# Swapping the 256-column and the 512-column matmuls inside three of the seven products of a Strassen pair

## The chip, the cores and the metric

The kernel runs on one core of one Trainium2 chip. The metric is device time in microseconds (us) for one execution; lower is better. Besides TensorE (PE), which runs the matmuls and loads their weights (PEld in the profile), the core has VectorE (DVE), ScalarE (ACT), GpSimd (POOL) and SyncE (SP), each with its own queue worked off in order, and 16 DMA engines.

## The reference

One layer of a token mixer over 512 frames of width 2048, in float32. One combined projection of the normalised input feeds three attention branches of four heads, and three gates; the branches are projected back, weighted by the gates, summed and projected once more.

```python
proj = jnp.einsum('bsd,dc->bsc', hn, w_in)            # 512 x 2048 by 2048 x 12292
br = proj[..., :QKVG_COLS].reshape(b, s, N_BRANCH, 4, BRANCH_W)      # q, k, v, gate path per branch
gates = jax.nn.sigmoid(proj[..., QKVG_COLS + N_HEADS:] + b_gate).reshape(b, s, N_BRANCH, D_MODEL)
...
ys = ys * jax.nn.silu(br[:, :, :, 3])                  # ys: the three branches' attention outputs
up = jnp.einsum('bsnw,nwd->bsnd', ys, w_up)
merged = jnp.sum(gates * up, axis=2)
return x + jnp.einsum('bsd,de->bse', merged, w_out)
```

Almost all of the arithmetic is in the two einsums with `w_in` and `w_out`, and the change is in how these are run.

## The kernel before

**Precision by two parts.** A float32 operand is cut into a high part (ACT copies it into a rounded type, line 244) and a low part (DVE subtracts the high part from the original, line 248). For weights these are the tiles `wh` and `wl`, each 128x1024, that is eight 128x128 blocks; for activations a tile `x`, `t` or `m` holds, for each of its halves, 256 high columns and then 256 low columns side by side. A product of a weight block and an activation half is then two matmuls, both issued at line 263:

- a **wide** one, `wh` by 512 columns (256 high, 256 low), into the whole of a PSUM tile `acc`,
- a **narrow** one, `wl` by the 256 high columns alone, into the left half of the same tile.

Left and right half of `acc` are added later.

**Seven products for a pair.** `PairTask` computes two output column tiles at once by a Strassen scheme: the contraction (2048) and the frames (512) are each cut in two, and seven products, numbered 1 to 7, take the place of eight. A product is eight weight blocks, so eight wide matmuls and eight narrow ones. The order of the products is

```python
self.order = (1, 5, 2, 3, 6, 7, 4) if late else (1, 2, 6, 5, 7, 3, 4)
```

All pairs but two have `late` false. In these, products 6, 7, 4 and 3 add onto the PSUM tile of an earlier product (`onto`, and with it `more` being true): 6 onto 1, 7 onto 6, 4 onto 7, 3 onto 5. The weights of product 6 are those of 1 plus those of 5 (a DVE add, line 626), and those of 3 are those of 2 plus that sum (line 632). There are 50 such pairs, 350 products: query, key, value and gate columns of eleven heads, most merge gates, and at the end the output projection. Activations `x` and `t` belong to the input projection, `m` to the output projection.

**What sets the order.** The kernel writes its own order for PE, ACT and DVE. A planner (`Flow`) holds generators; each yields an engine and an assumed cost, an event, or free slots, and the planner lets the one that could start first issue its next instruction. The main stream (`stream`) walks through the products one by one. When it comes to product i it starts `prep` of product i+2, which allocates `wh` and `wl` (three buffers of each) and yields the two splits. After a product, `after_of` reads the PSUM tile out. The attention of the heads (transposes at line 971 of the probabilities `p`, scores, values) is spread between as side work.

```python
def prep(u):
    n = u.shape[0] * P
    u.hi = wp.tile([P] + u.shape, F32R, tag="wh", name=nm("wh"), bufs=LA + 1)
    u.lo = wp.tile([P] + u.shape, F32R, tag="wl", name=nm("wl"), bufs=LA + 1)
    yield u.source_there()
    yield from split(u.hi, u.lo, u.source(), n, u.ready, hi_ev=u.ready_hi)
```

`ready_hi` is set after the ACT instruction, `ready` after the DVE one. `stream` waits for `ready_hi` ahead of a product, and the product itself waits for `ready` ahead of its narrow matmuls.

Of the kernel before, what the change touches and what calls it, by code (L numbers as in the profile page):

```python
# [16 lines left out]
S = 512  # L17
# [8 lines left out]
UK = 8  # L26
NQ = 4
HS = S // 2
# [8 lines left out]
PE, ACT, DVE = 0, 1, 2  # L37
# [112 lines left out]
def mm_us(n, x=1):  # L150
    return x * max(0.115, n / 2400 + 0.0133)
# [11 lines left out]
def hybrid_kernel(  # L163
# [40 lines left out]
    def acc(i=0):  # L204

        return pa.tile([P, S], F32, tag=f"acc{i}", name=nm("acc"), bufs=1 if i else 2)
# [10 lines left out]
    LH, RH = slice(0, HS), slice(HS, S)  # L217

    def two(ap):

        return ap.rearrange("p (h s) -> p h s", h=2)
# [40 lines left out]
    def mm(ps, w, x, start=False, stop=False, more=False):  # L262
        nc.tensor.matmul(ps, w, x, start=start, stop=stop, skip_group_check=more)  # L263
# [324 lines left out]
    class PairTask:  # L588
# [52 lines left out]
        def mms_of(self, i):  # L641
            p = self.order[i]
            bank = (0, 1, 2, 0, 0, 1, 2)[i] if self.late else {2: 1, 5: 2, 3: 2}.get(p, 0)
            onto = None if self.late else {6: 1, 7: 6, 4: 7, 3: 5}.get(p)
            more = onto is not None
            self.bank = getattr(self, "bank", {})
            self.bank[p] = bank

            def go(u):
                if more:  # L650
                    yield self.ev[onto]
                    self.ps[p] = self.ps[onto]
                else:
                    yield accs[bank], 1
                    self.ps[p] = acc(bank)

                for j in range(UK):
                    yield lambda: self.ops[p](j) is not None
                    r, _, ev = self.ops[p](j)
                    yield ev  # L660
                    yield PE, mm_us(S)
                    mm(two(self.ps[p]), u.hi[:, j, :], r, j == 0 and not more, more=more)
                yield u.ready
                for j in range(UK):
                    yield PE, mm_us(HS)
                    mm(self.ps[p][:, LH], u.lo[:, j, :], self.ops[p](j)[1], stop=j == UK - 1, more=more)
            return go

        def after_of(self, i):
# [875 lines left out]
```

## Time and profile before

| | |
|---|---|
| time, median of 3 runs | 1346.16 us (1345.8 to 1347.92) |
| the profiled execution: its time | 1346.45 us |
| the profiled execution: span of its instructions | 1344.7 us |
| granted TensorE clock, mean | 0.997 |
| PE busy | 1328.4 us, 7406 matmuls |
| DVE busy | 1112.7 us, 1624 instructions |
| ACT busy | 792.7 us, 1214 instructions |
| low splits of weights on DVE (line 248) | 412, 1200 ns each |
| high splits of weights on ACT (line 244) | 412, 1038 ns each |

The span runs from the first to the last instruction; the time is 1.75 us more. A matmul's row gives the time from its start until its result has been drained, and the next one starts before that: durations of matmuls overlap, and their pace is read from their starts. Where rows of a timeline are merged, `x8` behind a row is the number of instructions in it.

### The profile page before, as it was taken

The numbers are of one execution on the slowest core, as the hardware profiler recorded it, in microseconds if no ns is written. First come the engines' busy times: TensorE is split into PE (matmuls) and PEld (weight loads), VectorE is DVE, ScalarE is ACT, GpSimd is POOL, SyncE is SP. The second block draws the span as 40 slices with busy tenths as digits, with TensorE's granted clock in tenths as the row PEclk, the third lists the DMA queues.
The fourth block names the chain that finished last, engine by engine and source line by source line (L and its number), as shares of the span: only waits on it lengthen the run. The fifth ranks groups of instructions, "written<-read, shape, count | busy, mean of one in ns | idle before, by whom it ended". The sixth has DMA issues, their size and how long they took to land.

```text
span 1344.7 us, 19813 instructions
## 1 busy us (share of the span) xinstructions
PE 1328.4 (99%) x7406; PEld 1151.6 (86%) x7406; DVE 1112.7 (83%) x1624; ACT 792.7 (59%) x1214; POOL 91.3 (7%) x115
## 2 busy tenths in 40 slices
PE   9999999999999999999999999999999999989998
PEld 7788888888888888888888888888888788878887
DVE  5998998978888788787887878878798877898786
ACT  6745656656565566655766557665567655454443
POOL 0000000010000100000000000100000000001000
PEclk9999999999999999999999999999999999989999
DMA  9566767767777677777767777767767655658883
GB/s 328 176 154 158 190 165 195 181 188 203 186 200 195 180 215 182 185 206 184 214 171 190 203 194 199 176 191 198 194 193 257 238 197 188 187 146 242 235 250 91
DMA packets 91600, 263.03 MB, mean 196 GB/s; under 512 B 10216, under 2 KB 16488, under 8 KB 91504
## 3 DMA queue, kind: packets, MB, share of 16 engines
q1 hardware_dynamic: 72928, 202.97, 44.9%
q0 software_dynamic: 14976, 54.53, 24.8%
q10 hardware_dynamic: 3600, 4.26, 0.9%
q8 instruction: 58, 0.95, 0.3%
q14 instruction: 38, 0.31, 0.1%
HBM read 242.04 MB, written 19.69 MB: 195 GB/s over the span
## 4 chain that ended last, share of the span: by engine, by line
PE 97%; DVE 1%; DMA 0%; ACT 0%; issue 0%; SPq 0%; DVEq 0%; ACTq 0%
PE acc L263 84%; PE att L263 9%; PE att L971 1%; PE att L1074 1%; PE att L1075 1%; PE att L259 1%; PE att L260 1%; PE att L258 1%; DVE wl L248 1%; PE att L1073 1%; DMA x<-in_xT 0%; PE att L1034 0%; PE att L875 0%; PE att L874 0%; DVE m L248 0%; ACT wh L244 0%
## 5 line engine op out<-in xcount | busy, mean ns | idle before, releaser
L248 DVE TENSOR_TENSOR wl<-raw,wh 128x1024 fp32r<-128x1024 f32 (+1 forms) x412 | 494.2, 1200 | 146.8 <-ACT wh L244 144.3
L244 ACT ACTIVATE wh<-raw 128x1024 fp32r<-128x1024 f32 (+1 forms) x412 | 427.0, 1038 | 146.5 <-PE acc L263 70.8
L263 PE MATMUL acc<-x,wh 128*128 128x512 f32 x1600 | 415.5, 395 | 1.0 <-ACT wh L244 1.0
L263 PEld LDWEIGHTS acc<-x,wh 128*128 128x128 f32 x1600 | 286.0, 189 | 53.1 <-ACT wh L244 1.1
L263 PE MATMUL acc<-t,wh 128*128 128x512 f32 x1056 | 271.6, 394 | 0.0
L263 PEld LDWEIGHTS acc<-x,wl 128*128 128x128 f32 x1504 | 210.5, 190 | 19.0
L263 PE MATMUL acc<-x,wl 128*128 128x256 f32 (+1 forms) x1504 | 223.4, 289 | 0.0
L263 PEld LDWEIGHTS acc<-t,wh 128*128 128x128 f32 x1056 | 188.1, 189 | 32.1
L263 PEld LDWEIGHTS acc<-t,wl 128*128 128x128 f32 x1056 | 145.3, 190 | 11.0
L263 PE MATMUL acc<-t,wl 128*128 128x256 f32 x1056 | 149.2, 282 | 0.0
L279 POOL DMA_DIRECT2D raw<-in_w_col x88 | 76.1, 864 | 932.7 <-DMA raw<-in_w_col 446.5
L263 PE MATMUL acc<-m,wh 128*128 128x512 f32 x448 | 113.8, 396 | 6.3 <-DVE m L248 5.9
L263 PEld LDWEIGHTS acc<-m,wh 128*128 128x128 f32 x448 | 81.5, 191 | 21.6 <-DVE m L248 6.3
L742 ACT ACTIVATE c<-acc 128x256 f32<-128x256 f32 x50 | 19.2, 383 | 97.3 <-PE acc L263 92.2
L263 PE MATMUL att<-y,wh 128*128 128x512 f32 x256 | 66.5, 390 | 1.3 <-DVE y L248 1.3
L720 ACT ACTIVATE u<-acc 128x512 f32<-128x512 f32 x50 | 29.8, 595 | 64.3 <-PE acc L263 64.2
L263 PEld LDWEIGHTS acc<-m,wl 128*128 128x128 f32 x448 | 61.9, 193 | 5.2 <-DVE wl L248 0.8
L632 DVE TENSOR_TENSOR raw<-raw,raw 128x1024 f32<-128x1024 f32 x52 | 63.5, 1222 | 0.4
L626 DVE TENSOR_TENSOR raw<-raw,raw 128x1024 f32<-128x1024 f32 x52 | 63.4, 1220 | 0.4
L263 PE MATMUL acc<-m,wl 128*128 128x256 f32 x448 | 63.4, 285 | 0.4 <-DVE wl L248 0.4
L703 ACT ACTIVATE v<-acc 128x512 f32<-128x512 f32 x52 | 31.1, 599 | 50.8 <-PE acc L263 47.5
L263 PEld LDWEIGHTS att<-y,wh 128*128 128x128 f32 x256 | 47.9, 188 | 12.3 <-DVE y L248 2.5
(179 smaller groups left out, 1374.0 us busy)
## 6 DMA issues: line engine op xcount, KB each, us to landing
raw<-in_w_col SPq DMA_DIRECT2D x236, 512.0 KB, 4.3
raw<-in_w_col POOLq DMA_DIRECT2D x88, 512.0 KB, 6.3
raw<-in_w_out SPq DMA_DIRECT2D x40, 512.0 KB, 4.7
gl<-c SPq DMA_DIRECT2D x48, 256.0 KB, 2.2
raw<-in_w_up SPq DMA_DIRECT2D x32, 384.0 KB, 3.4
sg<-gl SPq DMA_DIRECT2D x48, 256.0 KB, 5.4
raw<-in_w_out POOLq DMA_DIRECT2D x16, 512.0 KB, 7.2
x<-in_xT SPq DMA_DIRECT2D x16, 256.0 KB, 6.8
```

Source lines behind the costliest of these rows:

```text
L244: nc.scalar.activation(hi, src, AF.Copy)
L248: nc.vector.tensor_sub(lo, src, f(hi))
L258: nc.tensor.matmul(ps, lh, rh, start=start, stop=False, skip_group_check=more)
L259: nc.tensor.matmul(ps, lh, rl, start=False, stop=False, skip_group_check=more)
L260: nc.tensor.matmul(ps, ll, rh, start=False, stop=stop, skip_group_check=more)
L263: nc.tensor.matmul(ps, w, x, start=start, stop=stop, skip_group_check=more)
L279: nc.gpsimd.dma_start(to, src, accum_op=ALU.add)
L626: nc.vector.tensor_add(w[1], w[1], w[5])
L632: nc.vector.tensor_add(w[2], w[2], w[1])
L703: nc.scalar.activation(self.v, ps, AF.Copy)
L720: nc.scalar.activation(self.u, ps, AF.Copy)
L742: nc.scalar.activation(c, ps[:, RH], AF.Copy, scale=-1.0)
```

## The change

In a pair that is not `late`, products 6, 7 and 4 run their eight narrow matmuls first and their eight wide ones last. Products 1, 2, 5 and 3 stay wide first. So product 2 (ending narrow) meets 6 (beginning narrow), 6 (ending wide) meets 5 (beginning wide), 5 meets 7 narrow to narrow, 7 meets 3 wide to wide, 3 meets 4 narrow to narrow, and 4 meets product 1 of the next pair wide to wide. Each of the three must now have its low split before its first matmul, where it needed the high split alone.

```diff
-                for j in range(UK):
-                    yield lambda: self.ops[p](j) is not None
-                    r, _, ev = self.ops[p](j)
-                    yield ev
-                    yield PE, mm_us(S)
-                    mm(two(self.ps[p]), u.hi[:, j, :], r, j == 0 and not more, more=more)
-                yield u.ready
-                for j in range(UK):
-                    yield PE, mm_us(HS)
-                    mm(self.ps[p][:, LH], u.lo[:, j, :], self.ops[p](j)[1], stop=j == UK - 1, more=more)
+                def wide(last):
+                    for j in range(UK):
+                        yield lambda: self.ops[p](j) is not None
+                        r, _, ev = self.ops[p](j)
+                        yield ev
+                        yield PE, mm_us(S)
+                        mm(two(self.ps[p]), u.hi[:, j, :], r, j == 0 and not more, last and j == UK - 1, more=more)
+
+                def narrow(last):
+                    yield u.ready
+                    for j in range(UK):
+                        yield lambda: self.ops[p](j) is not None
+                        _, r, ev = self.ops[p](j)
+                        yield ev
+                        yield PE, mm_us(HS)
+                        mm(self.ps[p][:, LH], u.lo[:, j, :], r, stop=last and j == UK - 1, more=more)
+                for step, last in ((narrow, False), (wide, True)) if p in (6, 7, 4) and more else (
+                        (wide, False), (narrow, True)):
+                    yield from step(last)
```

Nine lines are added above most of the code, so line 971 of before is line 980 of the changed kernel, and 712, 688, 1020 are 721, 697, 1029.

**An undisturbed junction.** On PE, around product 4 of an early pair (weights `wh_1420`, `wl_1421`; it ends that pair, and `wh_1446` begins the next one), the order before has narrow, wide, narrow, wide:

```order
L263 MATMUL acc_1392<-x_17_127,wl_1391 128x256
L263 MATMUL acc_1294<-t_120_960,wh_1420 128x512 x2
L263 MATMUL acc_1294<-t_124_980,wh_1420 128x512 x2
L263 MATMUL acc_1294<-t_129_1027,wh_1420 128x512 x2
L263 MATMUL acc_1294<-t_132_1037,wh_1420 128x512 x2
L263 MATMUL acc_1294<-t_120_960,wl_1421 128x256 x2
L263 MATMUL acc_1294<-t_124_980,wl_1421 128x256 x2
L263 MATMUL acc_1294<-t_129_1027,wl_1421 128x256 x2
L263 MATMUL acc_1294<-t_132_1037,wl_1421 128x256 x2
L263 MATMUL acc_1501<-x_2_112,wh_1446 128x512
```

In the changed kernel the same place on PE has narrow, narrow, wide, wide:

```order
L263 MATMUL acc_1392<-x_17_127,wl_1391 128x256
L263 MATMUL acc_1294<-t_120_960,wl_1421 128x256 x2
L263 MATMUL acc_1294<-t_124_980,wl_1421 128x256 x2
L263 MATMUL acc_1294<-t_129_1027,wl_1421 128x256 x2
L263 MATMUL acc_1294<-t_132_1037,wl_1421 128x256 x2
L263 MATMUL acc_1294<-t_120_960,wh_1420 128x512 x2
L263 MATMUL acc_1294<-t_124_980,wh_1420 128x512 x2
L263 MATMUL acc_1294<-t_129_1027,wh_1420 128x512 x2
L263 MATMUL acc_1294<-t_132_1037,wh_1420 128x512 x2
L263 MATMUL acc_1500<-x_2_112,wh_1446 128x512
```

Only the two groups of product 4 have changed places. Over the whole program the order of PE goes from narrow to wide at 387 places before and at 229 in the changed kernel, from wide to narrow at 388 and 231.

**An early product 6.** On DVE, ahead of the low split of one product 6 of the input projection (197 to 201 us in the profile of before; its low weights are `wl_296_1987` before), where `raw` are weights as loaded or summed, `u` and `c1` output tiles, and `p` the scores of a head:

```order
L626 TENSOR_TENSOR raw_266_1799<-raw_266_1799,raw_247_1656 128x1024
L1020 TENSOR_TENSOR p_235_1607<-p_235_1607,lk_273_1816 128x384
L248 TENSOR_TENSOR wl_301_2016<-raw_247_1656,wh_300_2015 128x1024
L712 TENSOR_TENSOR u_299_2014<-u_299_2014,acc_302_2017 128x512
L688 TENSOR_TENSOR c1_306_2049<-u_299_2014 128x256
L632 TENSOR_TENSOR raw_276_1840<-raw_276_1840,raw_266_1799 128x1024
L1020 TENSOR_TENSOR p_234_1606<-p_234_1606,lk_274_1819 128x512
L248 TENSOR_TENSOR wl_296_1987<-raw_266_1799,wh_295_1986 128x1024
```

The same place on DVE in the changed kernel, where these low weights are `wl_295_1981`:

```order
L1029 TENSOR_TENSOR p_233_1592<-p_233_1592,lk_275_1823 128x512
L626 TENSOR_TENSOR raw_267_1789<-raw_267_1789,raw_252_1679 128x1024
L248 TENSOR_TENSOR wl_301_2018<-raw_252_1679,wh_300_2017 128x1024
L721 TENSOR_TENSOR u_299_2016<-u_299_2016,acc_302_2019 128x512
L697 TENSOR_TENSOR c1_315_2067<-u_299_2016 128x256
L632 TENSOR_TENSOR raw_276_1835<-raw_276_1835,raw_267_1789 128x1024
L248 TENSOR_TENSOR wl_295_1981<-raw_267_1789,wh_294_1980 128x1024
```

The two steps on `p` now stand ahead of the add of line 626 (the 128x384 one further up, not in these rows); up to this low split the same instructions stand before it in both. On PE, at that product, the ten transposes of `p` stood between its wide and its narrow matmuls; in the changed kernel they stand ahead of both, and then come the narrow and after them the wide matmuls.

**The last product 6.** On PE, in the last pair (low weights `wl_13059`), before, at the two places where a width ends (the rows left out are the other blocks of the same groups):

```order
L263 MATMUL acc_13088<-m_2122_11754,wl_13035 128x256
L263 MATMUL acc_13060<-m_2114_11738,wh_13058 128x512
...
L263 MATMUL acc_13060<-m_2149_11901,wh_13058 128x512
L263 MATMUL acc_13060<-m_2114_11738,wl_13059 128x256
...
L263 MATMUL acc_13060<-m_2149_11901,wl_13059 128x256
L263 MATMUL acc_13138<-m_1916_10712,wh_13086 128x512
```

The same place on PE in the changed kernel:

```order
L263 MATMUL acc_13088<-m_2122_11754,wl_13035 128x256
L263 MATMUL acc_13060<-m_2114_11738,wl_13059 128x256
...
L263 MATMUL acc_13060<-m_2149_11901,wl_13059 128x256
L263 MATMUL acc_13060<-m_2114_11738,wh_13058 128x512
...
L263 MATMUL acc_13060<-m_2149_11901,wh_13058 128x512
L263 MATMUL acc_13138<-m_1916_10712,wh_13086 128x512
```

Here too the two groups have changed places; on DVE the order of the instructions is the same in both kernels around this product.

## Prediction

> **What bounds the kernel now.** I read the page first: engine shares, the slices and the chain that ended last.
>
> ```profile
> span 1344.7 us, 19813 instructions
> PE 1328.4 (99%) x7406; PEld 1151.6 (86%) x7406; DVE 1112.7 (83%) x1624; ACT 792.7 (59%) x1214; POOL 91.3 (7%) x115
> PEclk9999999999999999999999999999999999989999
> PE 97%; DVE 1%; DMA 0%; ACT 0%; issue 0%; SPq 0%; DVEq 0%; ACTq 0%
> ```
>
> PE is busy 99% at the full granted clock, and 97% of the chain is PE. So the time is the sum of the distances from one matmul's start to the next one's, plus the few places where PE waits. The waits of PE, each a single place except the second (two):
>
> ```profile
> PE acc L263 <- DVE m L248: 5.9, 1, 5.9
> PE acc L263 <- ACT wh L244: 1.4, 2, 1.0
> PE att L971 <- ACT p L1023: 1.4, 1, 1.4
> PE acc L263 <- DVE wl L248: 0.4, 1, 0.4
> ```
>
> The 5.9 us lie ahead of the output projection and the 1.0 of the second row is at the start; the change touches neither. The third row and the fourth matter below: both stand at a product 6, between its wide and its narrow matmuls.
>
> **What the junctions cost.** The timeline of PE over six undisturbed products, first a wide group, then a narrow one, and so on:
>
> ```profile
> 135.63 2.00 PE L263 MATMUL acc<-x,wh 128*128 128x512 f32 x8
> 137.47 1.12 PE L263 MATMUL acc<-x,wl 128*128 128x256 f32 x8
> 138.42 2.00 PE L263 MATMUL acc<-t,wh 128*128 128x512 f32 x8
> ...
> 152.39 2.00 PE L263 MATMUL acc<-t,wh 128*128 128x512 f32 x8
> ```
>
> By the starts, eight wide take 137.47 - 135.63 = 1.84 us, eight narrow 0.95, and a product (152.39 - 135.63) / 6 = 2.793. What equal widths in a row take is shown elsewhere. In the gated up-projection only wide matmuls follow each other; and two narrow ones that end a run of eight stand apart in this row, with the next group's start:
>
> ```profile
> 1122.91 1.98 PE L263 MATMUL att<-y,wh 128*128 128x512 f32 x8
> ...
> 1136.52 1.07 PE L263 MATMUL att<-y,wh 128*128 128x512 f32 x4
> ...
> 385.80 0.40 PE L263 MATMUL acc<-x,wl 128*128 128x256 f32 x2
> 386.04 2.00 PE L263 MATMUL acc<-x,wh 128*128 128x512 f32 x8
> ```
>
> From 1122.91 to 1136.52 there are 60 wide starts (groups of 8, 4, 8, 4, 4, 2, 4, 2, 8, 4, 8, 4): 13.61 / 60 = 0.2268 each, 1.815 for eight. The late narrow ones take 0.24 / 2 = 0.12 each, 0.96 for eight. So wide after narrow loses 1.84 - 1.815 = 0.025, narrow after wide gains 0.01, and a product without either would take 1.815 + 0.96 = 2.775, 0.018 less than 2.793. That is the price of one couple of junctions. [...]
>
> **The change, part by part.** Numbers and kinds of matmuls, splits and DMAs stay. First the junctions: by the order of PE there are 387 - 229 = 158 fewer from narrow to wide and 157 fewer the other way. About 15 of them lie ahead of 201 us, where DVE and not PE sets the pace (next part), so 143 count: 143 x 0.018 = **2.6 us saved**. Bounds: nothing, if a long narrow run makes the wide one pay twice (first rival); 143 x 0.021 = 3.0, if the roundings of the rows all err my way.
>
> Second, the low split is now needed at the start of products 6, 7 and 4, 1.84 us earlier. Where it is early by more than that, nothing waits. A usual pair's product 6, the tightest of the three (its low split on DVE, its start on PE):
>
> ```profile
> 490.50 1.22 DVE L248 TENSOR_TENSOR wl<-raw,wh 128x1024 fp32r<-128x1024 f32 x1
> 493.81 2.00 PE L263 MATMUL acc<-t,wh 128*128 128x512 f32 x8
> ```
>
> The split ends at 491.72, 2.09 us ahead of the first matmul. Laying the low splits against the products all through the trace, 146 of the 150 products concerned have over 1.2 us, one has 0.34 and three have less than none. One of these is the last row of the six products above: its split ends 0.12 late, at a place where the delay is taken up before 201 us. The other two are the waits of the second view. The first of them:
>
> ```profile
> 196.87 2.07 PE L263 MATMUL acc<-t,wh 128*128 128x512 f32 x8
> 198.78 0.49 PE L971 MATMUL att<-identf,p 128*128 128x128 f32 x3
> 199.88 2.35 DVE L248 TENSOR_TENSOR wl<-raw,wh 128x1024 fp32r<-128x1024 f32 x2
> 200.67 0.98 PE L971 MATMUL att<-identf,p 128*128 128x128 f32 x7 [1.40 <-ACT p L1023]
> 201.41 1.20 PE L263 MATMUL acc<-t,wl 128*128 128x256 f32 x8
> 202.45 0.63 PE L263 MATMUL acc<-x,wh 128*128 128x512 f32 x2
> 185.00:202.00 17.00, 16.47 (x22) 1.00 0.70 180
> ```
>
> The last row is of the busy times by stretch, for DVE: busy 16.47 of 17 us (behind it the clock and the DMA's share and GB/s), so the end of this low split, 199.88 + 1.22 = 201.1, is the end of a full DVE queue. Before, PE passes the time with the wide matmuls (1.84 us) and ten transposes. In the changed kernel DVE has the same work ahead of this split (the steps on `p` moved forward, the total did not), so PE can start the narrow group at about 201.1 and has all 2.79 us of the product still to do: next product at 203.9 in place of 202.45, 1.5 later. If the moved steps close what gaps DVE had (0.53 us), the split ends up to 0.4 sooner, so 1.1. I take **1.4 us lost**. The transposes now go into the wait and cost nothing. All that PE gained before 201 us is lost in it too. Queued behind the waiting matmul are only the following products; ACT and DVE fall back with PE and are not short of time after it.
>
> The second is the product 6 of the last pair, behind it the end:
>
> ```profile
> 1325.78 2.11 PE L263 MATMUL acc<-m,wh 128*128 128x512 f32 x8 [0.44 <-ACT wh L244]
> 1327.02 2.35 DVE L248 TENSOR_TENSOR wl<-raw,wh 128x1024 fp32r<-128x1024 f32 x2
> 1328.29 1.22 PE L263 MATMUL acc<-m,wl 128*128 128x256 f32 x8 [0.40 <-DVE wl L248]
> 1329.35 2.00 PE L263 MATMUL acc<-m,wh 128*128 128x512 f32 x8
> 1339.57 1.11 PE L263 MATMUL acc<-m,wl 128*128 128x256 f32 x8
> 1340.72 0.38 ACT L742 ACTIVATE c<-acc 128x256 f32<-128x256 f32 x1 [6.83 <-PE acc L263]
> ```
>
> DVE's order is the same here in both kernels, so the split still ends at 1327.02 + 1.22 = 1328.24. Narrow from 1328.29, then wide: next product at 1328.29 + 2.79 = 1331.08 in place of 1329.35, **1.7 us lost**; at least 1.3, if DVE gets there 0.4 earlier. It cannot be regained: what follows is PE alone.
>
> Third, the last matmul of all is now wide, and the last copy (1340.72) waits for it. A group's row lasts 2.00 - 1.84 = 0.16 us beyond its eight paces if wide and 1.11 - 0.95 = 0.16 if narrow, so the end stays where it was: nothing.
>
> Fourth, `wh` of products 6, 7 and 4 is now freed 0.95 us later and `wl` 1.84 earlier. The product three later gets that `wh` buffer: 3, the next pair's 1, the next 6. Its high split is not what ends last in the usual pair (product 6 keeps 2.09 us behind its low split, more than 0.95), so I cost this at nothing; what it costs without that cover is the third rival. DMAs, SP and POOL keep their order and have their old slack.
>
> Sum: 1.4 + 1.7 - 2.6 = +0.5 us on the profiled execution's 1346.45 (its span and 1.75 us around it). That execution is 0.29 above the median of the runs shown, so 1346.16 + 0.5 = **1346.7 us**. No change that a measurement can tell: 0.2% is 2.7 us, and the three runs spread over 2.1.
>
> **The rivals.** First, slower, by one mechanism: equal widths save nothing. The delay of wide after narrow is then a debt that the narrow matmuls run up (0.12 is more than half of 0.2268) and the wide ones pay, whichever order they stand in; sixteen narrow ones in a row would owe twice as much. Then only the losses stay: +3.1, **1349.3 us**. It decides if a couple saves less than 0.0028 us (3.1 - 143 x 0.0028 = 2.7). [...] Against it: within a run of eight narrow ones the last two already go at 0.12, the pace of the whole run (0.95 / 8), so no debt seems to be growing. Chance 0.19.
>
> Second, faster: the two waits do not lengthen, since the planner, which knows that the narrow group now comes first, has DVE and ACT reach these splits sooner. Then 1346.16 - 2.6 = **1343.6 us**, and 1343.2 with 3.0 saved, the only part of this case that is faster by over 0.2%. For it: at 201 us the order on DVE did change. Against it: the amount of work ahead of the split did not, and at 1328 us nothing changed. Chance 0.18.
>
> Third, slower too: the high buffers. ACT works in order, and its largest groups already idle for PE:
>
> ```profile
> L244 ACT ACTIVATE wh<-raw 128x1024 fp32r<-128x1024 f32 (+1 forms) x412 | 427.0, 1038 | 146.5 <-PE acc L263 70.8
> ```
>
> A high split that waits 0.95 us longer holds up all behind it on ACT, and through the add of line 626 the low split of product 6. If that slipped by more than its 2.09 us, by 0.1 us in each of some 43 input pairs, it would cost 4.3 us: 1346.7 + 4.3 = **1351.0 us**. Against it: 0.95 is under half of 2.09. Chance 0.07.
>
> **How the numbers follow.** The forecast has 0.56: 1346.7, from 1345.6 (3.0 saved, losses of 1.1 and 1.3) to 1349.3 (nothing saved). The range, 1343.4 to 1349.8, takes in the second rival's lower end nearly and the first one's value, and leaves out the third. Slower by over 0.2% (above 1348.9): the first rival, the third and 0.01 of the forecast, 0.27. Faster (under 1343.5): 0.09, half of the second rival. Within: 0.64.
>
> **What would show it.** In the changed profile, eight narrow after eight narrow take 0.96 and eight wide after eight wide 1.815, and the wide after sixteen narrow 1.84 again (first rival: 1.865). PE's waits at line 263 for DVE's `wl` number two, at about 201 and 1328 us, 2.5 to 4.5 us each; none of size at any other product 6. The prediction is wrong if the waits are shorter, if there are more of them, or if the junctions keep their price.

## The result, and the profile after

| | before | changed |
|---|---|---|
| median time (11 runs each) | 1346.42 us (1345.8 to 1347.92) | 1349.78 us (1347.78 to 1351.12) |
| profiled execution | 1346.45 us, span 1344.7 | 1349.19 us, span 1347.5 |

The ratio is 1.0025 with the interval 1.0018 to 1.0033: the changed kernel is 3.4 us slower. That lies at the upper end of the range forecast (1349.8) and just outside its likeliest case, "within 0.2%". One run of e8 further down (1638.62 us, granted clock 0.752) and one run of the kernel before beside e5 to e8 (2670.53 us) were slow and are left out of the ratios. The page of the changed kernel, with the span, the engine shares and the granted clock by slices:

```profile
span 1347.5 us, 19854 instructions
...
PE 1327.1 (98%) x7406; PEld 1154.1 (86%) x7406; DVE 1112.5 (83%) x1624; ACT 791.6 (59%) x1214; POOL 91.4 (7%) x115
...
PEclk9999999999999999999999999999999999989998
```

Two things are to be seen. PE is busy 1.3 us less although the span is 2.8 us longer: PE waits more. And the last digit of the clock's row is 8 where it was 9: at the end PE was granted less than its full clock. The waits of PE in the changed kernel:

```profile
PE acc L263 <- DVE m L248: 5.9, 1, 5.9
PE acc L263 <- DVE wl L248: 5.4, 2, 3.0
...
PE acc L263 <- ACT wh L244: 1.7, 1, 1.7
```

The second row is the two waits for a low split, and no third one exists. The wait for `p` of 1.4 us is gone. (The row for `wh` is at the start.) **The early product 6** of the changed kernel, in its timelines of PE and DVE:

```profile
199.46 2.35 DVE L248 TENSOR_TENSOR wl<-raw,wh 128x1024 fp32r<-128x1024 f32 x2
200.73 1.22 PE L263 MATMUL acc<-t,wl 128*128 128x256 f32 x8 [2.42 <-DVE wl L248]
...
204.09 1.99 PE L263 MATMUL acc<-x,wh 128*128 128x512 f32 x8
```

The split ends at 199.46 + 1.22 = 200.68, 0.4 sooner than before, and PE goes on at once. **The last pair's product 6** of the changed kernel and what is behind it: its low split on DVE's timeline, then PE's timeline:

```profile
1325.17 2.35 DVE L248 TENSOR_TENSOR wl<-raw,wh 128x1024 fp32r<-128x1024 f32 x2
1326.44 2.08 PE L263 MATMUL acc<-m,wl 128*128 128x256 f32 x8 [2.97 <-DVE wl L248]
1328.32 5.81 PE L263 MATMUL acc<-m,wh 128*128 128x512 f32 x16
1333.96 2.08 PE L263 MATMUL acc<-m,wl 128*128 128x256 f32 x16
1335.88 3.82 PE L263 MATMUL acc<-m,wh 128*128 128x512 f32 x16
1339.53 2.08 PE L263 MATMUL acc<-m,wl 128*128 128x256 f32 x16
```

The same time by stretches (their length, the busy time of PE, PEld, DVE, ACT and POOL, then the granted clock, the DMA's share and GB/s):

```profile
1322.34:1325.75 3.41, 1.14 (x9) 0.90 (x7) 2.75 (x4) 2.49 (x3) 0.00 (x0) 1.00 0.00 0
1325.75:1332.58 6.83, 6.13 (x18) 5.18 (x19) 1.77 (x2) 0.61 (x2) 0.00 (x0) 0.50 0.00 0
```

During the wait the clock goes to 0.50 for 6.83 us. The eight narrow matmuls behind it take 1328.32 - 1326.44 = 1.88 us (0.95 at full clock) and the sixteen wide ones 1333.96 - 1328.32 = 5.64 (1339.53 - 1335.88 = 3.65 for the next sixteen, at full clock). That is 0.93 + 1.99 = **2.9 us** that no step of the prediction contains.

**Where the time went.** Three products are followed by their starts on PE's timeline: one just behind the early wait, one in the gated up-projection, and one directly ahead of the last pair's product 6. First in the kernel before:

```profile
216.90 0.86 PE L263 MATMUL acc<-x,wh 128*128 128x512 f32 x3
...
1109.32 1.98 PE L263 MATMUL acc<-y,wh 128*128 128x512 f32 x8
...
1322.39 1.78 PE L263 MATMUL acc<-m,wh 128*128 128x512 f32 x7
```

And the same three in the changed kernel:

```profile
218.00 0.86 PE L263 MATMUL acc<-x,wh 128*128 128x512 f32 x3
...
1108.07 1.98 PE L263 MATMUL acc<-y,wh 128*128 128x512 f32 x8
...
1320.52 2.00 PE L263 MATMUL acc<-m,wh 128*128 128x512 f32 x8
```

The changed kernel is 1.10 late, then 1.25 ahead, then 1.87 ahead, and at the end of the span 2.8 late. So the early wait cost 1.1, the junctions of the input projection brought 1.10 + 1.25 = 2.35, and up to the last pair 1.87 - 1.25 = 0.62 more were gained. From there to the end 1.87 + 2.8 = 4.7 were lost: 2.9 to the half clock, and the other 1.8 to the wait.

Not all of the 0.62 is from junctions. The clock is at half behind the 5.9 us wait too, in both kernels, as the busy times by stretch show. The kernel before, the wait's middle and the drop:

```profile
1187.57:1190.98 3.41, 0.00 (x0) 0.00 (x0) 3.41 (x7) 0.23 (x1) 0.00 (x0) 1.00 0.68 173
1190.98:1197.81 6.83, 4.43 (x14) 3.86 (x15) 4.50 (x11) 1.47 (x2) 0.86 (x1) 0.50 0.85 212
```

The drop at that place in the changed kernel:

```profile
1189.22:1196.05 6.83, 3.92 (x13) 3.53 (x14) 4.54 (x9) 1.47 (x2) 0.86 (x1) 0.50 0.78 205
```

Of the 6.83 us PE works 4.43 before and 3.92 in the changed kernel. At half clock this is (4.43 - 3.92) / 2 = 0.25 less lost, and the junctions of the output projection have 0.37.

**The junctions** in the changed kernel, on PE's timeline at an early pair:

```profile
137.43 1.12 PE L263 MATMUL acc<-x,wl 128*128 128x256 f32 x8
138.38 1.12 PE L263 MATMUL acc<-t,wl 128*128 128x256 f32 x8
139.34 2.00 PE L263 MATMUL acc<-t,wh 128*128 128x512 f32 x8
141.18 1.98 PE L263 MATMUL acc<-x,wh 128*128 128x512 f32 x8
142.99 1.11 PE L263 MATMUL acc<-x,wl 128*128 128x256 f32 x8
```

Narrow after wide 0.95, narrow after narrow 0.96, wide after sixteen narrow 1.84, wide after wide 1.81.

### The profile page after: what moved, and what is told of

Same layout as the page of the kernel before. It is cut to its first block, busy times and chain, and to the rows that moved or that the text cites. A ratio compares the mean times of both kernels' runs of the same rounds, so it can differ in the third digit from the quotient of the medians.

```text
span 1347.5 us, 19854 instructions
## 1 busy us (share of the span) xinstructions
PE 1327.1 (98%) x7406; PEld 1154.1 (86%) x7406; DVE 1112.5 (83%) x1624; ACT 791.6 (59%) x1214; POOL 91.4 (7%) x115
## 4 chain that ended last, share of the span: by engine, by line
PE 97%; DVE 1%; DMA 0%; ACT 0%; issue 0%; SPq 0%; DVEq 0%; ACTq 0%
PE acc L263 84%; PE att L263 9%; PE att L980 1%; DVE wl L248 1%; PE att L1084 1%; PE att L1083 1%; PE att L259 1%; PE att L260 1%; PE att L258 1%; PE att L1082 1%; DMA x<-in_xT 0%; PE att L1043 0%; PE att L884 0%; PE att L883 0%; DVE m L248 0%; ACT wh L244 0%
## 5 line engine op out<-in xcount | busy, mean ns | idle before, releaser
L244 ACT ACTIVATE wh<-raw 128x1024 fp32r<-128x1024 f32 (+1 forms) x412 | 427.2, 1038 | 166.5 <-PE acc L263 91.7
L263 PEld LDWEIGHTS acc<-x,wh 128*128 128x128 f32 x1600 | 294.2, 188 | 61.8 <-ACT wh L244 1.9
L263 PE MATMUL acc<-t,wh 128*128 128x512 f32 x1056 | 268.2, 393 | 0.0
L263 PE MATMUL acc<-t,wl 128*128 128x256 f32 x1056 | 153.4, 285 | 2.5 <-DVE wl L248 2.4
L263 PEld LDWEIGHTS acc<-t,wl 128*128 128x128 f32 x1056 | 138.4, 192 | 3.4 <-DVE wl L248 2.7
L263 PEld LDWEIGHTS acc<-m,wh 128*128 128x128 f32 x448 | 84.2, 194 | 22.6 <-DVE m L248 6.3
```

The source lines that it names most:

```text
L244: nc.scalar.activation(hi, src, AF.Copy)
```

## The experiments

The theory after the result: a wait of PE costs its length, and beyond that the granted clock can fall to 0.50, from inside the wait (at 1325.75 in the changed kernel) or shortly behind it (at 201.50 in e1), for 6.83 us in the first case and 3.41 in the second. In the traces it falls at borders between stretches of 3.41 us. The two drops shown of the changed kernel start 1325.75 - 1189.22 = 136.53 us apart, and 136.53 / 40 = 3.413. Its clock falls once more behind the last matmul, at 1346.23, 157.01 us after the first drop; in the kernel before it falls at 1190.98 and, again behind the last matmul, at 1344.58, 153.60 us apart: 46.0 and 45.0 times 3.413. A rival: the waits alone and something else in the new order make the tail long. In all kernels below pairs have a number (4 is the pair of the early wait, 51 the last, 44 the first of the output projection), by which the edits choose their place.

**e1: the last pair's product 6 wide first again.**

```diff
-  if p in (6, 7, 4) and more else
+  if p in (6, 7, 4) and (self.number, p) != (51, 6) and more else
```

> The changed kernel, but product 6 of the last pair is wide first again. Theory (clock): the 2.97 us wait of PE ahead of that product's narrow group costs 1.7 us as a wait and some 2.9 us more because the granted clock is 0.5 for 6.8 us from inside it; without it the time is that of before, less 3.0 for the junctions, plus 1.1 for the wait at 201 us: about 1344.6 us, granted clock 0.997 in every run. Rival (wait alone): the half clock is not caused by the wait and stays; only the 1.7 us go: about 1348.1 us. Rival (junctions save nothing): about 1347.5 us, since only the wait at 201 us is left.

Measured: 1345.99 us (1344.54 to 1346.96; before 1346.08), ratio 0.9997, interval 0.9988 to 1.0006. The 3.8 us came back, but 1.4 fewer than expected. The times fall in two groups, four of 1344.5 to 1345.2 at a mean clock of 0.997, as expected, and seven of 1345.7 to 1347.0 at 0.996. The profiled run (1346.57) is of the second, and its timeline of PE shows the early wait:

```profile
201.00 1.69 PE L263 MATMUL acc<-t,wl 128*128 128x256 f32 x8 [2.42 <-DVE wl L248]
```

By stretches, in e1:

```profile
198.08:201.50 3.42, 1.00 (x9) 0.77 (x8) 3.39 (x5) 1.92 (x5) 0.00 (x0) 1.00 0.56 164
201.50:204.91 3.41, 3.41 (x14) 2.82 (x13) 2.18 (x5) 0.00 (x0) 0.00 (x0) 0.50 0.81 255
```

The same wait by stretches in the changed kernel's profiled run:

```profile
195.94:199.35 3.41, 2.37 (x20) 2.10 (x18) 3.27 (x4) 3.41 (x7) 0.00 (x0) 1.00 0.87 195
199.35:202.77 3.42, 2.04 (x13) 1.87 (x14) 3.42 (x5) 0.38 (x2) 0.00 (x0) 1.00 0.51 165
```

In both PE waits 2.42 us. In e1 one stretch holds all of it (idle 3.42 - 1.00 = 2.42) and the clock halves at its end, 0.5 us after PE has begun again. In the changed kernel a border at 199.35 divides it into 1.04 and 1.38, and the clock stays. So not the wait's length alone decides, but also how the borders of that trace divide it (198.08 and 201.50 in e1, 199.35 in the changed kernel). In e1 the drop cost about 1.6 us: from PE's start behind the wait to the next product it is 205.91 - 201.00 = 4.91 us, in the changed kernel 204.09 - 200.73 = 3.36.

**e2: the kernel before with only the last pair's product 6 narrow first.**

```diff
-  if p in (6, 7, 4) and more else
+  if (self.number, p) == (51, 6) and more else
```

> The kernel before, with only product 6 of the last pair narrow first. Theory (clock): one product of 350 carries nearly the whole loss and more: 1346.4 + 1.7 + 2.9 = about 1351.0 us, with a granted clock of 0.993 to 0.995. Rival (wait alone): 1346.4 + 1.7 = 1348.1 us at a clock of 0.997.

Measured: 1347.91 us (1347.45 to 1351.28), ratio 1.0023, interval 1.0014 to 1.0032. Both expectations came true, in turn: six runs of 1347.4 to 1347.9 at a mean clock of 0.997 or more, five of 1350.4 to 1351.3 at 0.994 to 0.996. The profiled run is of the first group; PE's timeline at its last wait:

```profile
1327.96 1.22 PE L263 MATMUL acc<-m,wl 128*128 128x256 f32 x8 [2.96 <-DVE wl L248]
```

And the stretches there, in e2:

```profile
1323.25:1326.67 3.42, 1.76 (x12) 1.44 (x10) 2.53 (x4) 3.09 (x4) 0.00 (x0) 1.00 0.11 38
1326.67:1330.08 3.41, 2.12 (x13) 1.94 (x14) 2.37 (x3) 0.00 (x0) 0.00 (x0) 1.00 0.02 5
```

A wait of 2.96 us, as long as the changed kernel's 2.97, but divided by a border at 1326.67 into idle parts of 1.66 and 1.29: no drop, and the tail lost 1.8 us, what the prediction priced at 1.7.

**e3: the changed kernel with work in the last wait.** 48 matmuls whose result nothing reads stand ahead of the last product 6. They add work, and DVE's split is due no sooner.

```diff
+  if (self.number, p) == (51, 6):
+      yield atts, 1
+      yield PE, 0.1
+      d = att()
+      for _ in range(48):
+          nc.tensor.matmul(d[:, :P], identb, identb, start=True, stop=True)
+      give(atts)
```

> The changed kernel with 48 matmuls of 128 columns on a spare PSUM tile, whose result nobody reads, put on PE ahead of the narrow group of the last pair's product 6, where PE waits for 2.97 us. The wait for the low split stays, PE is busy in it. Theory (clock): the clock stays at 1.0, the 2.9 us go and the 1.7 us stay: 1349.8 - 2.9 = about 1346.9 us. Rival (wait alone): nothing changes, 1349.8 us, or more if the added matmuls outlast the wait.

Measured: 1346.92 us (1346.59 to 1348.67), ratio 1.0008, interval 1.0 to 1.0017: adding 48 matmuls made the kernel 2.9 us faster (2.5 if each is taken against the kernel before run beside it). Six runs lie at 1346.6 to 1346.9, five (the profiled one among them) at 1348.3 to 1348.7, with the early wait's drop as in e1 in its trace (0.50 from 201.66 to 205.07); the two groups are 1.7 us apart. The last wait of e3, filled, on PE's timeline:

```profile
1325.45 2.85 PE L666 MATMUL att<-identb 128*128 128x128 bf16 x48
1328.58 1.22 PE L263 MATMUL acc<-m,wl 128*128 128x256 f32 x8 [0.27 <-DVE wl L248]
1329.63 3.82 PE L263 MATMUL acc<-m,wh 128*128 128x512 f32 x16
```

Eight narrow now take 1329.63 - 1328.58 = 1.05 where they took 1.88. The place and the end of the wait stayed; only PE's idleness went. The rival falls.

**e4: both late products 6 wide first again,** the other 148 products narrow first.

```diff
+  if p in (6, 7, 4) and (self.number, p) not in ((51, 6), (4, 6)) and more else
```

> The changed kernel with both late products 6, the one at 201 us and the last pair's, wide first again; the other 148 products stay narrow first. Theory: only the junctions are left, 143 couples less the three beside the two products at 0.021 us: 1346.4 - 3.0 = about 1343.4 us, 1.1 under the kernel with only the last one undone. Rival (junctions save nothing): 1346.4 us.

Measured: **1343.31 us** (1342.22 to 1344.51; before 1346.08), ratio 0.9978, interval 0.9969 to 0.9987, as expected: without the two waits the junctions are a gain. Around the early product 6 PE waits little, and the wait for `p` that the kernel before has there is gone too, since this plan, like that of the changed kernel, has the steps on `p` further forward (PE's timeline of e4):

```profile
198.04 2.07 PE L263 MATMUL acc<-t,wh 128*128 128x512 f32 x8
200.71 1.21 PE L263 MATMUL acc<-t,wl 128*128 128x256 f32 x8 [0.59 <-DVE wl L248]
```

Not all of the lead is from junctions. Of the 3.1 us by which e4's span is shorter in the profiled runs, 0.78 is there at 216 us already: the product that starts at 216.90 before starts at 216.12 in e4. Ahead of the 5.9 us wait the lead is 3.08, so the junctions up to there are worth 2.3, as in the changed kernel.

**e5: both waits of the changed kernel filled,** with 44 such matmuls in the early one too (into a free PSUM tile `acc`). **e8: the same with 24 in place of 48 in the last wait,** which leaves about half of it open. The core of the edit, e5 against e3 and then e8 against e5:

```diff
-  if (self.number, p) == (51, 6):
+  fill = {(51, 6): (48, 1), (4, 6): (44, 0)}.get((self.number, p))
...
-  fill = {(51, 6): (48, 1), (4, 6): (44, 0)}.get((self.number, p))
+  fill = {(51, 6): (24, 1), (4, 6): (44, 0)}.get((self.number, p))
```

> The changed kernel, all 150 products narrow first, with unread matmuls of 128 columns in both waits: 44 ahead of the narrow group at 201 us, 48 ahead of the last pair's. Both waits for the low split stay. Theory (clock): no half clock is left that the kernel before does not have, and what stays is what the prediction priced: junctions -3.0, waits +1.0 and +1.75, so about 1346.1 to 1346.6 us in all runs, without a second group of times above. Rival (the wait at 201 us costs more by itself): like the kernel with the last wait alone filled, 1346.9 us with a second group at 1348.5.

> As the kernel with both waits filled, but with 24 in place of 48 unread matmuls in the last wait, so that PE is idle there for some 1.6 us in one piece. In the profiles so far the clock fell at the end of a stretch of 3.41 us with 2.28 us or more of idle PE in it, and never with 1.66 us or less. Theory (threshold): 1.6 us do not reach it, so the time is that of both filled, 1346.1 to 1346.6 us. Rival (each idle stretch costs clock in proportion): about half of the 2.9 us, 1347.7 us.

e5: 1346.88 us (1345.97 to 1347.45; before 1346.51), ratio 1.0003, interval 0.9994 to 1.0012, all runs in one group. That is 0.3 above what was expected, and 0.4 above the kernel before, which the interval can't tell from nothing: without a drop at either wait the change agrees with what the prediction's sum says, +0.5. e8: 1347.15 us, ratio 1.0007, interval 0.9998 to 1.0016; eight runs at 1346.4 to 1347.7 and two at 1348.9 to 1349.2. The profiled run is one of these two, and by its stretches the drop is not at the tail:

```profile
8.56:11.97 3.41, 1.55 (x7) 1.18 (x8) 2.71 (x5) 2.37 (x4) 0.00 (x0) 1.00 1.07 379
11.97:15.38 3.41, 3.41 (x10) 2.25 (x9) 3.06 (x6) 3.41 (x8) 0.00 (x0) 0.50 1.03 365
...
1326.10:1329.52 3.42, 1.81 (x27) 1.59 (x27) 3.39 (x5) 1.59 (x2) 0.00 (x0) 1.00 0.00 0
```

1.86 us idle in a stretch at the start of the kernel are followed by a drop, 1.61 us at the tail are not. e8's median lies between its two expectations (1346.6 and 1347.7) and decides nothing by itself; its trace does.

**e11: the kernel before with only the early product 6 narrow first.**

```diff
-  if p in (6, 7, 4) and more else
+  if (self.number, p) == (4, 6) and more else
```

> The kernel before with the early product 6 alone narrow first (the one at 201 us), everything else as before. Wait alone: the first matmul waits for the low weight's tile about 1.0 to 1.4 us longer than before, so about 1347.3 in one group. Clock theory: the same, but in some runs the idle stretch takes over half of a 3.41 us window and the clock falls to half behind it, which adds 1.7 to 1.8 us: a second group of runs at about 1349.

Measured: 1351.31 us (1349.75 to 1351.94; before 1346.49), ratio 1.0035, interval 1.0023 to 1.0047. More than either group expected, and none of the six runs is in the first group. The profiled run, on PE's timeline:

```profile
200.74 1.76 PE L984 MATMUL att<-identf,p 128*128 128x128 f32 x7 [3.11 <-ACT p L1036]
```

And its stretches:

```profile
196.21:199.63 3.42, 1.41 (x11) 1.00 (x9) 3.39 (x5) 1.98 (x3) 0.00 (x0) 1.00 0.95 226
199.63:206.46 6.83, 5.72 (x23) 5.33 (x24) 4.25 (x7) 2.73 (x6) 0.00 (x0) 0.50 0.53 181
```

Here the plan kept the order of `p` that the kernel before has, and the transposes wait 3.11 us for it. A stretch idle for 3.42 - 1.41 = 2.01 us was enough, and the half clock lasted 6.83 us, not the 3.41 that the expectation had taken from e1. What each cost is an estimate from the starts: from these transposes to the narrow matmuls of the next product it is 209.27 - 200.74 = 8.53 us. In the kernel before it is 204.76 - 200.67 = 4.09, and a wide group (1.84) has come to stand in this stretch, so 5.93 at full clock. The half clock is then worth 2.6 us. These narrow matmuls start 209.27 - 204.76 = 4.5 later than before, so the wait alone is worth 1.9, where 1.0 to 1.4 were expected.

**e6, e7, e9, e10: work in the 5.9 us wait, misplaced.** Before (e6, e9) and e4 (e7, e10) got 104 such matmuls, meant for the wait ahead of the output projection; e6 and e7 placed them in product 4 of the first output pair, e9 and e10 in its product 7.

```diff
+  if (self.number, p, j) == (44, 7, UK - 1):
+      yield atts, 1
+      yield PE, 0.1
+      d = att()
+      for _ in range(104):
+          nc.tensor.matmul(d[:, :P], identb, identb, start=True, stop=True)
+      give(atts)
```

> The kernel before, with 104 unread matmuls of 128 columns on PE in its longest wait, 5.9 us for DVE's split of m ahead of the output projection, behind which the clock is half for 6.8 us in every profile so far. Theory (clock): some 4.6 us of work run at half speed there, so 2.3 us go: about 1343.8 us. Rival: the clock falls there for another reason, and the time stays at 1346.1 us.

> The changed kernel with the two late products 6 wide first, and with the same 104 unread matmuls in the 5.9 us wait. Theory: the two gains add, 1343.3 - 2.3 = about 1341.0 us, under both kernels. Rival: they overlap, 1343.3 us.

> The kernel before with 104 unread 128-column matmuls put into its longest TensorE wait, the 5.9 us ahead of the last block of product 7 of the first output pair. Clock theory (an idle stretch lets the granted clock fall to half for a fixed time afterwards): the half clock of 6.83 us from 1190.98 goes; of it about 4.6 us are matmul work that took twice its time, so 2.3 us are saved: about 1344.0 where the kernel before gives 1346.3, and no row of half clock between 1185 and 1200. Rival (the clock falls there for another reason, or the fill outlasts the wait): 1346.3 or more, with the half clock still there or the block starting late.

> The changed kernel with both late products 6 wide first again, and the same 104 unread matmuls in the 5.9 us wait. Clock theory: what e4 gave (1343.3) less 2.3: about 1341.0, faster than both kernels. Rival (the two gains overlap, or the saved time is given back in the next wait for the first output tile): 1343.3.

Measured: 1352.18, 1349.47, 1352.17 and 1349.24 us (before 1346.51 in the first two, 1346.49 in the others), all slower than the kernel they were put in, by 5.5 to 5.7 if each is taken against the kernel before run beside it. In e9 they came behind the wait, by PE's timeline:

```profile
1193.38 0.80 PE L263 MATMUL acc<-m,wh 128*128 128x512 f32 x1 [5.87 <-DVE m L248]
1193.97 1.91 PE L263 MATMUL acc<-m,wl 128*128 128x256 f32 x8
1195.68 2.75 PE L263 MATMUL acc<-m,wh 128*128 128x512 f32 x7
1198.27 5.98 PE L670 MATMUL att<-identb 128*128 128x128 bf16 x104
```

The wait belongs to product 6, as this pair is `late` and runs its products in the other order. The four say nothing on the clock. In e9 the next matmul starts at 1204.06, so the 104 take 1204.06 - 1198.27 = 5.79 us, 0.0557 each: outside a wait nearly all of that is lost.

**e12: e10 with 96 of them in product 6, that is e4 with the 5.9 us wait filled.**

```diff
-  if (self.number, p, j) == (44, 7, UK - 1):
+  if (self.number, p, j) == (44, 6, UK - 1):
...
-      for _ in range(104):
+      for _ in range(96):
```

> The changed kernel with both late products 6 wide first again, and 96 unread 128-column matmuls (96 x 0.0556 = 5.3 us by their pace of 0.0556 in e10) at the place where TensorE waits 5.87 us, ahead of the last block of product 6 of the first output pair (in e9 and e10 the same matmuls stood one product behind it, outside the wait). Clock theory: the wait is filled, no half clock follows it, and the 2.3 us that were lost there are saved: e4's 1343.3 - 2.3 = about 1341.0, with no wait over 1 us at that place. Rival (the clock falls there for another reason): 1343.3. If the matmuls outlast the wait: 1343.3 or more.

Measured: **1341.22 us** (1340.98 to 1341.53; before 1346.29), ratio 0.9963, interval 0.995 to 0.9977: faster than both kernels. Against the kernel before run beside it, it is 5.1 us ahead, and e4 was 2.8 ahead: the filled wait is worth 2.3, as expected. The place on e12's timeline of PE:

```profile
1184.81 5.53 PE L670 MATMUL att<-identb 128*128 128x128 bf16 x96
1190.84 0.50 PE L263 MATMUL acc<-m,wh 128*128 128x512 f32 x1 [0.49 <-DVE m L248]
1191.17 1.12 PE L263 MATMUL acc<-m,wl 128*128 128x256 f32 x8
1192.13 2.00 PE L263 MATMUL acc<-m,wh 128*128 128x512 f32 x8
```

And the clock's row on its page:

```profile
PEclk9999999999999999999999999999999999999999
```

The wait still ends when DVE is done, but the matmuls behind it run at full pace from the first one on (eight narrow in 0.96 us, in e9 with the drop 1195.68 - 1193.97 = 1.71), and the 8 in the clock's row is gone.

## Why the prediction came out as it did

**Inside the range by luck.** The measured 1349.78 us lies within the range up to 1349.8, but that end was chosen to take in the first rival, which is false, as shown next. The forecast itself was +0.5 us, the measured change is +3.4, and the half clock that makes the difference in the profiled run is in no term of the sum and in none of the rivals. The likeliest case, within 0.2% with a chance of 0.64, did not come.

**The junctions: right, mechanism and size.** Forecast 2.6 us, measured 2.35 up to the up-projection and 0.37 in the output projection, 2.7. The wide group after sixteen narrow ones takes the 1.84 us of a wide group after eight; the first rival would have had 1.865 and no gain. That rival had nearly the right total (1349.3) for a wrong reason: by it e4 could be faster than before only by what the early wait brings (0.8 in the profiled runs), and the junctions bring 2.3 more there up to the 5.9 us wait.

**The early wait: right within its bounds.** Forecast 1.4 (1.1 to 1.5), measured 1.1: DVE reached the split 0.4 sooner, the lower bound. That is this run's: in the profiled run of e5, with the same order and no drop, the split ends at 201.07, as late as before, and the next product's narrow matmuls start 206.31 - 204.76 = 1.55 late. The wait is 2.42 us, a shade under the 2.5 to 4.5 announced. That the planner would remove both waits, the second rival, did not happen; it removed the one for `p`, which the prediction had seen go into the new wait.

**The last wait: right in its place and length, wrong in its price.** The split ends at 1325.17 + 1.22 = 1326.39 and the narrow group starts 0.05 us later, as forecast, and PE loses 1.8 us by waiting, as in e2. The step that failed is the sentence "**1.7 us lost**; at least 1.3": it priced idle time by its length. The idle time also lowered the clock (to 0.50; with work in the wait, in e3, it stays at 1.00), and that was worth 2.9 us more in the profiled run. The profiled execution came out 1349.19 - 1346.45 = 2.7 us later, nearly this one term, since the smaller early wait (0.3) and the shorter drop behind the 5.9 us wait (0.25) offset most of the forecast's own 0.5. Part of the same failed step is the early wait, "**1.4 us lost**": the changed kernel's profiled run has no drop there, but e1 shows one, worth 1.6 us. That a run can have one, the other or both would explain why the changed kernel's runs spread over 3.3 us where those of before spread over 2.1. Their mean clocks fit, 0.996 in the fastest run and 0.993 in the slowest, but only one of them has a trace.

The profile of before did hold a warning: the 8 in the clock's row, at the 5.9 us wait. The prediction read it as "PE is busy 99% at the full granted clock" and put no price on it. Its own wait of 1.4 us for `p` had been followed by no drop (clock 1.00 from 195 to 205 us); the shortest idle time that one followed in these traces is 1.86 us.

**The high buffers: as forecast.** ACT waits longer for PE to free them, in the changed kernel:

```profile
L244 ACT ACTIVATE wh<-raw 128x1024 fp32r<-128x1024 f32 (+1 forms) x412 | 427.2, 1038 | 166.5 <-PE acc L263 91.7
```

91.7 us in place of 70.8, and no PE wait for `wh` or `wl` in any usual pair came of it. The third rival did not occur.

**The end: as forecast.** Ending on a wide group instead of a narrow one moved the end by less than 0.1 us against the last product's start.

## What to carry to other kernels

Price a new wait of the busiest engine twice: its length, and, if TensorE is idle for around 1.9 us or more of some 3.41 us stretch (here 1.86 us were followed by a drop, 1.66 were not), what the half clock takes from the work behind it, here 1.6 us (e1) to 2.9 us (the changed kernel's tail). A reordering that gains 0.02 us at each of 143 places is undone by one or two such waits, so undo it at just these places (two of 150 products here turned +3.4 into -2.8 us, some 0.8 of it by the gone wait for `p`). Where a wait cannot be removed, unread matmuls inside it can keep the clock up: 48 in the last wait (e3) and 96 in the 5.87 us one (e12) did, at 1.00, and cost nothing that the times show; they left 0.27 and 0.49 us of the waits open.

## What the runs showed of the hardware

In these traces the granted clock falls to 0.50 at the end of a 3.41 us stretch in which PE idled for 1.86 us or more, and stays there for one or two stretches (3.41 us in e1 and e8; 6.83 at the tail and in e11). Idle times per stretch that were followed by a drop are 1.86 (e8), 2.01 (e11), 2.27 (tail of the changed kernel) and 2.42 us (e1); those that were not are 1.66 (e2), 1.61 (e8) and 1.38 (changed kernel). So the border lies between 1.66 and 1.86 us in these traces, about half of the stretch, as far as the profile's busy times are exact. In both cases of 3.41 us shown here PE was busy for the whole of the first half-clock stretch (3.41 of 3.41 in e1 and e8); where it idled for a part of it (6.83 - 6.13 = 0.7 at the tail, 1.1 in e11) the half clock went on for a second one. None of the four stretches with a drop just named was idle as a whole; in the kernel before, the stretch from 1187.57, ahead of its drop at 1190.98, is.

The borders lie differently in different traces (at the tail 1325.75 in the changed kernel, 1326.67 in e2, 1326.10 in e8). That they do so between runs of one kernel too would explain the two groups of times (e2: 1347.4 to 1347.9 and 1350.4 to 1351.3); one run of each kernel was traced, so this is argued and not shown. What sets the choice between one and two stretches of half clock was read from traces alone and not tried. Nor was it separated why a wide group after a narrow one takes 0.025 us longer; the traces show only that it takes 1.84 us after eight narrow matmuls and after sixteen, and 1.81 behind a wide group.
